# Moving a background matrix-vector product to other units of a hand-scheduled transformer kernel

## The chip, the core and the metric

The kernel runs on one core of one Trainium2 chip. The metric is device time in microseconds (us) of one execution, taken as the median of three runs. A profiled execution has a time of its own, and a span from its first to its last instruction.

## What is computed

Two transformer blocks run over 256 tokens of width 2048, all in float32. The first has a stick-breaking attention layer and a latent attention layer. The second has a gated convolution, a sparse attention that picks 64 keys for each query, and a feed-forward part. The second block is modulated by six vectors that depend on a condition `c` alone:

```
mod = silu(c) @ w_ada + b_ada                    # w_ada is 2048 x 12288
sh1, sc1, gt1, sh2, sc2, gt2 = split(mod, 6)
h = rms_norm(x, g_pre_mix) * (1 + sc1) + sh1     # then the projections, convolution, attention
x = x + gt1 * rms_norm(mixed, g_post_mix)
h = rms_norm(x, g_pre_ffn) * (1 + sc2) + sh2     # then the feed-forward part
x = x + gt2 * rms_norm(f, g_post_ffn)
```

The modulation needs nothing of the token stream, so its 100 MB of weights can be read at any time before the vectors are used.

## The kernel before, in words

**Units.** The class `Run` writes out the whole program in the order of units. A unit (`u`) is 6 matmuls of 128x128 by 128x512 on the TensorE (PE) for one half `t` of the tokens: each weight is split into a high and a low part, and two slices of 128 rows take three matmuls each. A block is 512 columns of one weight matrix, 16 units where it has 2048 rows. `pump` brings weights in, up to 10 units ahead: SyncE (SP) issues a load of 512 KB into one of 4 buffers `wst` for each two units, ScalarE (ACT) makes the high part `wh` and VectorE (DVE) the low part `wl` (L213 and L214, or L227 and L228 where a gain is folded in). There are 6 buffers of `wh` and of `wl`, so a `wl` can be made at most 12 units ahead of the matmuls that read it.

**Side work.** After each unit `side` advances generators that hold everything else: norms, transposes (L522, which DVE and ACT then split into `h` and `l` tiles such as `ah` and `al`), attention heads, the convolution. A generator's `yield n` says that its next piece is written n units later. Each engine runs its own instructions strictly in the order of writing, so what is written first also waits first.

**The modulation products.** At the end of `side` stands the modulation. It has 384 slices of `w_ada` (128 rows by 512 columns, 256 KB). GpSimd (POOL) issues the load of one into one of 3 buffers `ast` (L329), and DVE multiplies it with one value of silu(c) for each row and adds it to `ada` (L571, or L568 for the first of 16). After 16 slices `ada_sum` adds up the partitions: ACT and DVE split `ada` into `adh` and `adl`, and 5 units later PE multiplies them with ones (L588, L589). `spread` gives each slice a due unit, evenly over the units that it calls calm: away from the turns between stages (`turns`) and from a stretch named by `heads`. Of the 384 slices, 320 have their place ahead of the feed-forward part. In `side`, one unit uses a slice or begins a load, not both (`elif`), and a load begins only when one of the three buffers has been used.

**Stages, in order of time.** First layer's projections and stick-breaking heads (units 0 to 271), output projection `w_out_a` (272 to 335), a turn with the short matrix `w_ple_proj` and then `w_ple_gate` (336 to 407); the latent stage with `w_dkv`, `w_in_b`, and the pairs `w_uk`, `w_uv`, `w_uq` with latent attention (408 to 575); `w_out_b` and the second turn of that kind (576 to 711); the second block's `w_in` with convolution and sparse attention (712 to 1111), `w_o` (1112 to 1175), and the feed-forward part. At the entries to the second block and to the feed-forward part, `affine` turns the normed rows of each half into the transposed activation, four pieces of 512 columns for each half, in `to_c` and `to_f`.

**Places that the change touches.** `side`; `mix_sums`, called in `out_phase`, which forms three sums for the norm after `w_o` (L556 on ACT, L1692 on DVE, L1693 on ACT); `to_c`; `conv`, 31 DVE operations for each of 8 groups of channels (L1393, L1396), written four at a time with 3 units between; `spread`.

Of the kernel before, what the change touches and what calls it, by code (L numbers as in the profile page):

```python
# [29 lines left out]
XBUF = 3  # L30
# [4 lines left out]
CONV_PACE = 3  # L35
# [100 lines left out]
class Run:  # L136
# [170 lines left out]
    def side(self):  # L307
        for rec in list(self.urgent):
            if not rec[2] and rec[1] <= self.u:
                self.advance(rec)  # L310
        for rec in self.slow:
            if rec[1] <= self.u:
                self.advance(rec)
        self.urgent, self.slow, self.active = ([r for r in x if not r[2]] for x in (self.urgent, self.slow, self.active))
        if (self.queue and len(self.active) < self.width and self.u >= self.last + self.space
                and all(r[2] for r in self.queue[0][3])):
            rec = self.queue.popleft()
            rec[1] = self.u
            self.active.append(rec)
            self.last = self.u  # L320
        self.step()
        if self.xc < self.xd and self.extra[self.xc][0] <= self.u:
            x = self.extra[self.xc]
            x[2](x[3])
            self.xc += 1
        elif (self.xd < len(self.extra) and self.xd - self.xc < XBUF and self.extra[self.xd][0] - 12 <= self.u):
            x = self.extra[self.xd]
            st = self.main.tile([P, NB], F32, tag="ast", bufs=XBUF, name="ast")
            self.nc.gpsimd.dma_start(st, x[1])  # L329
            x.append(st)  # L330
            self.xd += 1
# [111 lines left out]
def body(ctx, tc, a, out):  # L443
# [192 lines left out]
    blocks = []  # L636
# [278 lines left out]
    def out_phase(w, act_in, begin, src, act_next, then, sums=None, last_groups=None):  # L915


        def enter():
            st["x"], st["og"], st["oss"] = {}, {}, {}
            begin()  # L920
            for t in range(2):
                st["x"][t] = ph.tile([P, D], tag="x", bufs=2)
                nc.gpsimd.dma_start(st["x"][t], src(t))

        def epi_of(j):
            def epi(t, acc):
                if j == 0:
                    st["og"][t] = wide()
                    st["oss"][t] = small(ph.pool, 12, "oss")
                square(acc, st["oss"][t][:, j : j + 1])  # L930
                sl = slice(j * NB, (j + 1) * NB)
                nc.vector.tensor_tensor(st["og"][t][:, sl], acc, st["gp"][:, sl], op=ALU.mult)
                if sums is not None:
                    sums(t, j, st["og"][t][:, sl])
                if j == 3:

                    def fin():
                        r = rstd_of(ph.pool, total(ph.pool, st["oss"][t][:, 0:4]), D)
                        x = st["x"][t]

                        def update(g):
                            s2 = slice(g * NB, (g + 1) * NB)
                            nc.vector.scalar_tensor_tensor(x[:, s2], st["og"][t][:, s2], r, x[:, s2],
                                                           op0=ALU.mult, op1=ALU.add)
                            return x[:, s2]

                        yield from then(t, r, update)

                    run.advance(run.add(fin(), act_next, t))
                yield 1  # L950

            return epi

        for j in range(4):
            add_block(w, (0, D), j * NB, NB, act_in, epi_of(j), spare=j > 0 or act_in is not actB2,
                      groups=last_groups if j == 3 else None, enter=phase("po", enter) if j == 0 else None)
# [373 lines left out]
    def to_c(t, j, x):  # L1330
# [3 lines left out]
        if j == 3:  # L1334
            if t == 0:
                gain_of(0, "mix")
            x, xn = st["x"][t], wide()
            r = rstd_of(ph.pool, total(ph.pool, st["xss", t]), D)

            def norm(g):  # L1340
                sl = slice(g * NB, (g + 1) * NB)
                nc.vector.tensor_scalar(xn[:, sl], x[:, sl], r, None, op0=ALU.mult)
                return xn[:, sl]

            yield from affine(t, actC, 0, norm, *TO_C[t])
# [45 lines left out]
    def conv(c):  # L1391
        u, acc = st["uT"][:, c, :], st["cacc"][:, c, :]
        nc.vector.tensor_scalar(acc, u, wdw[:, c, 30:31], col("bdw", c), op0=ALU.mult, op1=ALU.add)  # L1393
        for k in range(29, -1, -1):
            sft = 30 - k
            nc.vector.scalar_tensor_tensor(acc[:, sft:], u[:, : S - sft], wdw[:, c, k : k + 1], acc[:, sft:],  # L1396
                                           op0=ALU.mult, op1=ALU.add)
            if k % 4 == 0:
                yield CONV_PACE

    def conv_chain(j, before):
        while not all(r[2] for r in before):
# [460 lines left out]
    def spread(run):  # L1863
# [1 line left out]
        uf = blocks[n_ffn].u0  # L1865
        calm = lambda lo, hi: [u for u in range(lo, hi) if all(not b - 12 <= u < b + 20 for b in turns)
                               and not heads[0] - 4 <= u < heads[-1] + 4]
        heads = [b.u0 for b in blocks if b.w.tensor.name in (a["w_uk"].tensor.name, a["w_uq"].tensor.name)]
        turns = [b.u0 for b in blocks if b.enter is not None or b.ahead is not None or b.w.tensor.name == a["w_ple_proj"].tensor.name]
        xs = []  # L1870
        uc = conv_block.u0
        for qs, us in ((range(20), calm(100, uc - 30) + calm(uc + 290, uf - 110)), (range(20, 24), calm(uf + 40, uf + 300))):
            todo = [(q, k) for q in qs for k in range(16)]
            for i, (q, k) in enumerate(todo):
                xs.append([us[len(us) * i // len(todo)], *ada_chunk(q, k)])
# [53 lines left out]
```

## Time and profile before

| | before |
|---|---|
| median of 3 runs | 2538.36 us (2535.8 to 2538.81) |
| profiled execution's own time | 2536.7 us |
| its span | 2534.9 us |
| PE busy | 2471.3 us, 97% |
| DVE busy | 1814.5 us, 72% |
| ACT busy | 1329.5 us, 52% |
| POOL busy | 283.6 us, 11% |
| mean granted TensorE clock | 0.994 |

Busy is the time in which an engine has an instruction running. The ends of matmuls are modelled and overlap, so a busy PE says that no gap was seen, and what a stage could gain is read from PE's gaps and from the stretches at the lower clock. Waits are put down to the instruction that came last.

### The profile page before, as it was taken

To read this page: it belongs to the slowest core of one execution; us is meant where nothing else is said; L and a number is where in the kernel's file an instruction comes from. 1 tells how busy PE (TensorE), PEld (TensorE's weight loads), DVE (VectorE), ACT (ScalarE), POOL (GpSimd) and SP (SyncE) were. 2 spreads that over 40 slices of the span, in tenths; PEclk is the share of its full clock that TensorE was granted. 3 is DMA by queue.
4 is the path that set the end of the run, shared out by engine and by line. 5 is a ranking of instruction groups with operands and counts; after the bars stand their busy time and mean duration, and the time that the engine had idled before them with its cause. 6 is when DMAs were issued, how large, how long until landed. Compare 5 with 4: busy or idle time off the path is not lost.

```text
span 2534.9 us, 33034 instructions
## 1 busy us (share of the span) xinstructions
PE 2471.3 (97%) x11818; PEld 2051.2 (81%) x11818; DVE 1814.5 (72%) x2492; ACT 1329.5 (52%) x1938; POOL 283.6 (11%) x535
## 2 busy tenths in 40 slices
PE   9999999999899999999999999999999999999998
PEld 7888888878689887878977877888788878888886
DVE  5466677787776667767999867675776787776665
ACT  6555564455555555554544465445644554455453
POOL 2011112112213401000000001100000000000000
PEclk9999999999999999999999999999999999999999
DMA  7577778887786667756656547875577767656563
GB/s 250 172 237 251 253 233 297 283 270 247 264 277 193 195 220 250 230 194 191 188 150 198 176 150 225 286 257 192 176 265 259 238 200 269 223 181 228 184 202 126
DMA packets 272213, 562.51 MB, mean 222 GB/s; under 512 B 20984, under 2 KB 43928, under 8 KB 270000
## 3 DMA queue, kind: packets, MB, share of 16 engines
q1 hardware_dynamic: 236688, 438.56, 53.6%
q0 software_dynamic: 34448, 120.67, 13.9%
q8 instruction: 93, 1.52, 0.2%
q10 hardware_dynamic: 912, 1.17, 0.1%
q14 instruction: 72, 0.59, 0.1%
HBM read 551.86 MB, written 8.45 MB: 221 GB/s over the span
## 4 chain that ended last, share of the span: by engine, by line
PE 85%; DVE 6%; DMA 3%; ACT 2%; issue 2%; POOL 1%; DVEq 0%; POOLq 0%; SPq 0%; ACTq 0%
PE acc L421 17%; PE acc L423 17%; PE acc L422 17%; PE acc L344 7%; PE sc L421 5%; PE sc L423 5%; PE sc L422 5%; PE sc L344 4%; PE pv L344 3%; DVE wl L214 2%; DMA ast<-in_w_ada_dram 2%; PE sc L1205 1%; PE tp L522 1%; ACT wh L213 1%; PE pv L1205 1%
## 5 line engine op out<-in xcount | busy, mean ns | idle before, releaser
L214 DVE TENSOR_TENSOR wl<-wst,wh 128x1024 fp32r<-128x1024 f32 (+2 forms) x758 | 904.3, 1198 | 447.8 <-ACT wh L213 444.6
L213 ACT ACTIVATE wh<-wst 128x1024 fp32r<-128x1024 f32 (+2 forms) x758 | 783.8, 1038 | 728.1 <-PE acc L423 289.2
L421 PE MATMUL acc<-wh,ah 128*128 128x512 f32 (+4 forms) x1630 | 639.8, 393 | 5.6 <-ACT wide L1600 2.9
L422 PE MATMUL acc<-wl,ah 128*128 128x512 f32 (+4 forms) x1630 | 628.0, 385 | 1.5 <-DVE wl L214 1.5
L423 PE MATMUL acc<-wh,al 128*128 128x512 f32 (+4 forms) x1630 | 627.5, 385 | 1.9 <-DVE sst L551 1.9
L329 POOL DMA_DIRECT2D ast<-in_w_ada_dram x384 | 207.7, 541 | 1514.5 <-DVE ada L571 1262.6
L421 PEld LDWEIGHTS acc<-wh,ah 128*128 128x128 f32 x1630 | 308.9, 190 | 64.7 <-ACT wide L1600 3.4
L423 PEld LDWEIGHTS acc<-wh,al 128*128 128x128 f32 x1630 | 308.5, 189 | 62.2 <-DVE al L527 2.1
L422 PEld LDWEIGHTS acc<-wl,ah 128*128 128x128 f32 x1630 | 309.1, 190 | 57.1 <-DVE wl L214 3.3
L571 DVE SCALAR_TENSOR_TENSOR ada<-ast,silu_c,ada 128x512 f32<-128x512 f32 x360 | 268.2, 745 | 61.8 <-DMA ast<-in_w_ada_dram 61.7
L1396 DVE SCALAR_TENSOR_TENSOR cv<-cv,wdw 128x255 f32<-128x255 f32 (+14 forms) x240 | 112.3, 468 | 6.5
L344 PE MATMUL acc<-wh,ah 128*128 128x512 f32 x270 | 105.6, 391 | 0.0
L344 PE MATMUL acc<-wh,al 128*128 128x512 f32 x270 | 105.1, 389 | 0.0
L344 PE MATMUL acc<-wl,ah 128*128 128x512 f32 x270 | 105.1, 389 | 0.0
L421 PE MATMUL sc<-wh,ah 128*128 128x512 f32 x266 | 104.7, 394 | 0.0
L422 PE MATMUL sc<-wl,ah 128*128 128x512 f32 x266 | 103.7, 390 | 0.0
L423 PE MATMUL sc<-wh,al 128*128 128x512 f32 x266 | 103.7, 390 | 0.0
L227 ACT ACTIVATE wh<-wst,cols 128x512 fp32r<-128x512 f32 (+2 forms) x112 | 68.3, 663 | 43.5 <-PE acc L423 27.5
L228 DVE SCALAR_TENSOR_TENSOR wl<-wst,cols,wh 128x512 fp32r<-128x512 f32 (+2 forms) x112 | 72.2, 688 | 13.8 <-ACT wh L227 13.7
L421 PE MATMUL sc<-wh,hh 128*128 128x512 f32 x176 | 68.9, 391 | 0.0
L421 PE MATMUL acc<-wh,hh 128*128 128x512 f32 x176 | 68.8, 391 | 0.0
L423 PE MATMUL acc<-wh,hl 128*128 128x512 f32 x176 | 68.5, 389 | 0.0
(440 smaller groups left out, 3892.1 us busy)
## 6 DMA issues: line engine op xcount, KB each, us to landing
ast<-in_w_ada_dram POOLq DMA_DIRECT2D x384, 256.0 KB, 4.2
wst<-in_w_in_dram SPq DMA_DIRECT2D x144, 512.0 KB
wst<-in_w_in_a_dram SPq DMA_DIRECT2D x120, 512.0 KB
wst<-in_w_down_dram SPq DMA_DIRECT2D x88, 512.0 KB
wst<-in_w_gate_dram SPq DMA_DIRECT2D x70, 512.0 KB
wst<-in_w_up_dram SPq DMA_DIRECT2D x70, 512.0 KB
wst<-in_w_ple_gate_dram SPq DMA_DIRECT2D x64, 512.0 KB
wst<-in_w_in_b_dram SPq DMA_DIRECT2D x40, 512.0 KB
```

The costliest lines, as they stand in the source:

```text
L213: nc.scalar.activation(wh, st, AF.Copy)
L214: nc.vector.tensor_sub(wl, st, wh.bitcast(F32))
L227: nc.scalar.activation(wh[:, c, :], st[:, c, :], AF.Copy, scale=g)
L228: nc.vector.scalar_tensor_tensor(wl[:, c, :], st[:, c, :], g, wh[:, c, :].bitcast(F32), op0=ALU.mult, op1=ALU.subtract)
L329: self.nc.gpsimd.dma_start(st, x[1])
L344: nc.tensor.matmul(banks[x], lhsT=l, rhs=r[:, c, :], start=new and c == k == 0, stop=stop and c == 1 and k == 2, skip_group_check=True)
L421: nc.tensor.matmul(o, lhsT=hi, rhs=wh[:, c, :], start=kc == 0, stop=False)
L422: nc.tensor.matmul(o, lhsT=hi, rhs=wl[:, c, :], start=False, stop=False)
L423: nc.tensor.matmul(o, lhsT=lo, rhs=wh[:, c, :], start=False, stop=kc == b.cp * b.np - 1)
L571: nc.vector.scalar_tensor_tensor(acc, w, s, acc, op0=ALU.mult, op1=ALU.add)
L1205: nc.tensor.matmul(o, lhsT=l, rhs=r, start=start, stop=True, skip_group_check=True)
L1396: nc.vector.scalar_tensor_tensor(acc[:, sft:], u[:, : S - sft], wdw[:, c, k : k + 1], acc[:, sft:], op0=ALU.mult, op1=ALU.add)
```

## The change

Five places change. `side` may use a slice and begin a load in one unit. `spread` counts the whole latent stage, from `w_dkv` on, as not calm (before, only from `w_uk` on), and lets the products begin at unit 66 in place of 100. In `out_phase` and in `to_c`, the last piece of the second half's sums is written one unit later. `conv` writes two operations at a time, with 2 units and 1 unit between in turn.

```
 in side:
             x[2](x[3])
             self.xc += 1
-        elif (self.xd < len(self.extra) and self.xd - self.xc < XBUF and self.extra[self.xd][0] - 12 <= self.u):
+        if (self.xd < len(self.extra) and self.xd - self.xc < XBUF and self.extra[self.xd][0] - 12 <= self.u):
...
 in out_phase:
                 if sums is not None:
+                    if j == 3 and t == 1:
+                        yield 1
                     sums(t, j, st["og"][t][:, sl])
...
 in to_c:
             if t == 0:
                 gain_of(0, "mix")
+            else:
+                yield 1
...
 in conv:
-            if k % 4 == 0:
-                yield CONV_PACE
+            if k % 2 == 0:
+                yield 2 if k % 4 == 0 else CONV_PACE - 2
...
 in spread:
-        heads = [b.u0 for b in blocks if b.w.tensor.name in (a["w_uk"].tensor.name, a["w_uq"].tensor.name)]
+        heads = [b.u0 for b in blocks if b.w.tensor.name in (a["w_dkv"].tensor.name, a["w_uq"].tensor.name)]
...
-        for qs, us in ((range(20), calm(100, uc - 30) + calm(uc + 290, uf - 110)), (range(20, 24), calm(uf + 40, uf + 300))):
+        for qs, us in ((range(20), calm(66, uc - 30) + calm(uc + 290, uf - 110)), (range(20, 24), calm(uf + 40, uf + 300))):
```

With the constants of the kernel, `spread` has 406 calm units for the 320 slices before and 376 after. They are, after: 66 to 259, 292 to 323, 362 to 395, 560 to 563, 596 to 627, 666 to 681, 1002 to 1065. Before, the list began at 100 and also held 428 to 491. Since a use and a load took a unit each, the program before could place one slice in two units only, and it fell behind its due units by up to 91 of them; after the change each slice stands in its due unit.

DVE at the entry of the latent stage, before: the weights of `w_dkv` (L228), the last update of `x` by the gate (L977, L978), the split of the transposed `x` (L527) and the statistics of the next norm (L551, L542).

```order
L977 TENSOR_TENSOR nat<-nat,big 128x512
L978 TENSOR_TENSOR x<-x,nat 128x512
L571 SCALAR_TENSOR_TENSOR ada<-ast,silu_c,ada 128x512
L228 SCALAR_TENSOR_TENSOR wl<-wst,cols,wh 128x320 x2
L527 TENSOR_TENSOR al<-tp,ah 128x512
L571 SCALAR_TENSOR_TENSOR ada<-ast,silu_c,ada 128x512
L228 SCALAR_TENSOR_TENSOR wl<-wst,cols,wh 128x320 x2
L551 TENSOR_REDUCE sst_5550<-xss_4812 128x1
L542 TENSOR_SCALAR var_5552<-sst_5550 128x1
L527 TENSOR_TENSOR al<-tp,ah 128x512
```

The same place now (line numbers behind L329 are 2 to 4 higher):

```order
L979 TENSOR_TENSOR nat<-nat,big 128x512
L980 TENSOR_TENSOR x<-x,nat 128x512
L228 SCALAR_TENSOR_TENSOR wl<-wst,cols,wh 128x320 x2
L527 TENSOR_TENSOR al<-tp,ah 128x512
L228 SCALAR_TENSOR_TENSOR wl<-wst,cols,wh 128x320 x2
L551 TENSOR_REDUCE sst_5829<-xss_5105 128x1
L542 TENSOR_SCALAR var_5831<-sst_5829 128x1
L527 TENSOR_TENSOR al<-tp,ah 128x512
```

The products (L571) no longer stand between the steps that lead to the latent stage; no L571 stands on DVE from there to the last of `w_uq`.

DVE in the middle of `w_out_a`, before, where a product stands behind each `wl`:

```order
L571 SCALAR_TENSOR_TENSOR ada<-ast,silu_c,ada 128x512
L214 TENSOR_TENSOR wl<-wst,wh 128x1024
L585 TENSOR_TENSOR adl<-ada,adh 128x256
L571 SCALAR_TENSOR_TENSOR ada<-ast,silu_c,ada 128x512
L214 TENSOR_TENSOR wl<-wst,wh 128x1024
L571 SCALAR_TENSOR_TENSOR ada<-ast,silu_c,ada 128x512
L214 TENSOR_TENSOR wl<-wst,wh 128x1024
```

And now:

```order
L585 TENSOR_TENSOR adl<-ada,adh 128x256
L571 SCALAR_TENSOR_TENSOR ada<-ast,silu_c,ada 128x512 x2
L214 TENSOR_TENSOR wl<-wst,wh 128x1024
L571 SCALAR_TENSOR_TENSOR ada<-ast,silu_c,ada 128x512 x2
L214 TENSOR_TENSOR wl<-wst,wh 128x1024
L571 SCALAR_TENSOR_TENSOR ada<-ast,silu_c,ada 128x512
L214 TENSOR_TENSOR wl<-wst,wh 128x1024
```

Most `wl` now have two products between them. ACT at the entry of the feed-forward part, before: the second half's sums (L556 of `sc`, L556 of `wide`, L1693) and the first half's second and third piece of `affine` (L1316, L1319).

```order
L556 ACTIVATE junk,oss_15567<-sc 128x512
L556 ACTIVATE junk,oss_15567<-wide 128x512
L1693 ACTIVATE nat,oss_15567<-nat 128x512
L1316 ACTIVATE nat<-tp,mods,gsc 128x128 x4
L1319 ACTIVATE ah<-nat 128x512
L213 ACTIVATE wh<-wst 128x1024 x2
L1316 ACTIVATE nat<-tp,mods,gsc 128x128 x4
```

And now:

```order
L556 ACTIVATE junk,oss_15567<-sc 128x512
L1318 ACTIVATE nat<-tp,mods,gsc 128x128 x4
L1321 ACTIVATE ah<-nat 128x512
L213 ACTIVATE wh<-wst 128x1024
L556 ACTIVATE junk,oss_15567<-wide 128x512
L1697 ACTIVATE nat,oss_15567<-nat 128x512
L213 ACTIVATE wh<-wst 128x1024
L1318 ACTIVATE nat<-tp,mods,gsc 128x128 x4
```

The two sums went from ahead of the second piece to between the second and the third.

## Rows read from the trace of the kernel before

**Rows 1.** The page: each engine's busy time, its share of the span, instructions.

```profile
PE 2471.3 (97%) x11818; PEld 2051.2 (81%) x11818; DVE 1814.5 (72%) x2492; ACT 1329.5 (52%) x1938; POOL 283.6 (11%) x535
```

**Rows 2.** Stretches: us, busy of PE, PEld, DVE, ACT, POOL, clock, DMA share, GB/s.

```profile
600.00:900.00 300.00, 280.83 (x1685) 247.53 (x1684) 199.98 (x366) 168.14 (x354) 87.10 (x170) 0.98 0.70 223
650.00:700.00 50.00, 43.01 (x177) 34.37 (x178) 36.91 (x72) 29.70 (x66) 14.64 (x33) 0.90 0.76 248
437.00:492.00 55.00, 55.00 (x247) 45.57 (x247) 41.23 (x52) 25.14 (x36) 10.23 (x19) 1.00 0.93 335
492.00:523.00 31.00, 27.17 (x133) 21.36 (x132) 24.52 (x36) 18.60 (x30) 5.73 (x11) 1.00 0.65 214
990.00:1016.00 26.00, 21.50 (x106) 16.89 (x105) 23.04 (x34) 17.14 (x26) 5.27 (x9) 1.00 0.69 233
1250.00:1350.00 100.00, 100.00 (x483) 79.14 (x482) 92.54 (x193) 47.61 (x70) 0.00 (x0) 1.00 0.55 163
1350.00:1360.00 10.00, 7.06 (x24) 5.39 (x24) 9.68 (x17) 5.16 (x6) 0.00 (x0) 0.83 0.67 206
```

**Rows 3.** PE's waits from 600 to 900 us: total, times, longest.

```profile
PE acc L421 <- DVE kT L1124: 3.6, 4, 1.3
PE tp L522 <- DVE ckvl L535: 2.5, 1, 2.5
PE acc L423 <- DVE sst L551: 1.9, 1, 1.9
```

**Rows 4.** DVE in order of time: start, length; in brackets idle time before, and releaser.

```profile
626.20 0.75 DVE L571 SCALAR_TENSOR_TENSOR ada<-ast,silu_c,ada 128x512 f32<-128x512 f32 x1 [5.79 <-DMA ast<-in_w_ada_dram]
...
628.04 0.68 DVE L527 TENSOR_TENSOR al<-tp,ah 128x512 fp32r<-128x512 f32 x1
...
640.25 0.75 DVE L571 SCALAR_TENSOR_TENSOR ada<-ast,silu_c,ada 128x512 f32<-128x512 f32 x1 [1.14 <-DMA ast<-in_w_ada_dram]
```

**Rows 5.** POOL in order of time, 618 to 642 us.

```profile
618.11 0.54 POOL L986 DMA_DIRECT2D spill<-x  x1 [0.81 <-DVE x L978]
618.64 0.55 POOL L329 DMA_DIRECT2D ast<-in_w_ada_dram  x1
...
641.30 0.54 POOL L329 DMA_DIRECT2D ast<-in_w_ada_dram  x1 [2.61 <-DVE ada L571]
```

**Rows 6.** The chain, in order of time: one load of a slice, and 6 matmuls.

```profile
618.64 7.46 DMA ast<-in_w_ada_dram
...
1886.50 1.36 PE sc L344 x6
```

**Rows 7.** Products from 611 to 870 us, and DVE's idle time before them.

```profile
L571 DVE SCALAR_TENSOR_TENSOR ada<-ast,silu_c,ada x71: 736/745/760, 612.5 to 868.9; 128x512 f32<-128x512 f32 x71
...
  DMA ast<-in_w_ada_dram: 44.0, 16
```

**Rows 8.** PE's waits over the whole span, one row.

```profile
PE tp L522 <- DVE x L943: 5.5, 6, 1.2
```

**Rows 9.** Loads of slices from 700 to 740 us, from issue to landing.

```profile
DMA to landing us min/median/max: 3.6/4.2/5.4
```

**Rows 10.** Products and loads of slices from 454 to 480 us.

```profile
L571 DVE SCALAR_TENSOR_TENSOR ada<-ast,silu_c,ada x12: 742/746/752, 454.3 to 478.8; 128x512 f32<-128x512 f32 x12
...
DMA to landing us min/median/max: 4.0/5.2/6.0
```

**Rows 11.** One of DVE's groups from 437 to 492 us: busy, mean, idle before.

```profile
L571 DVE SCALAR_TENSOR_TENSOR ada<-ast,silu_c,ada 128x512 f32<-128x512 f32 x19 | 14.2, 747 | 9.0 <-DMA ast<-in_w_ada_dram 9.0
```

**Rows 12.** Products from 144 to 397 us.

```profile
L571 DVE SCALAR_TENSOR_TENSOR ada<-ast,silu_c,ada x75: 736/745/752, 145.9 to 391.6; 128x512 f32<-128x512 f32 x75
```

**Rows 13.** Entry of the feed-forward part, in order of time: ACT twice, then PE.

```profile
1791.40 0.63 ACT L556 ACTIVATE junk<-wide 128x512 bf16<-128x512 f32 x1 [2.92 <-DVE wide L932]
...
1792.76 1.49 ACT L1316 ACTIVATE nat<-tp,mods,gsc 128x128 f32<-128x128 f32 x4
...
1794.96 0.50 PE L421 MATMUL acc<-awh,ah 128*128 128x512 f32 x1 [3.38 <-ACT ah L1319]
```

More of the change, by code (lines that the diff above doesn't have):

```diff
@@ L325, in side @@
             self.xc += 1
-        elif (self.xd < len(self.extra) and self.xd - self.xc < XBUF and self.extra[self.xd][0] - 12 <= self.u):
+        if (self.xd < len(self.extra) and self.xd - self.xc < XBUF and self.extra[self.xd][0] - 12 <= self.u):
             x = self.extra[self.xd]
@@ L933, in epi @@
                 if sums is not None:
+                    if j == 3 and t == 1:
+                        yield 1
                     sums(t, j, st["og"][t][:, sl])
@@ L1336, in to_c @@
                 gain_of(0, "mix")
+            else:
+                yield 1
             x, xn = st["x"][t], wide()
@@ L1397, in conv @@
                                            op0=ALU.mult, op1=ALU.add)
-            if k % 4 == 0:
-                yield CONV_PACE
+            if k % 2 == 0:
+                yield 2 if k % 4 == 0 else CONV_PACE - 2
     def conv_chain(j, before):
@@ L1867, in spread @@
                                and not heads[0] - 4 <= u < heads[-1] + 4]
-        heads = [b.u0 for b in blocks if b.w.tensor.name in (a["w_uk"].tensor.name, a["w_uq"].tensor.name)]
+        heads = [b.u0 for b in blocks if b.w.tensor.name in (a["w_dkv"].tensor.name, a["w_uq"].tensor.name)]
         turns = [b.u0 for b in blocks if b.enter is not None or b.ahead is not None or b.w.tensor.name == a["w_ple_proj"].tensor.name]
@@ L1871, in spread @@
         uc = conv_block.u0
-        for qs, us in ((range(20), calm(100, uc - 30) + calm(uc + 290, uf - 110)), (range(20, 24), calm(uf + 40, uf + 300))):
+        for qs, us in ((range(20), calm(66, uc - 30) + calm(uc + 290, uf - 110)), (range(20, 24), calm(uf + 40, uf + 300))):
             todo = [(q, k) for q in qs for k in range(16)]
```

## The prediction

> **What bounds the kernel now.** I read the page first: PE has an instruction running in 97% of the span, no other engine in more than 72% [rows 1]. So time can come back only where PE has gaps or runs at the lower clock. The view of stretches shows where these are. From 600 to 900 us, the latent stage, PE is busy for 280.83 of 300 us, a gap of 19.2 us, and between 650 and 700 us the granted clock is 0.90, so 10 of these 50 us ran at the lower of the two levels and 5.0 us of work were lost [rows 2]. Two more gaps lie at the turns to `w_ple_proj`: 31.00 - 27.17 = 3.8 us and 26.00 - 21.50 = 4.5 us [rows 2]. A matmul stretch without a gap looks like 437 to 492 us, 55.00 of 55.00 [rows 2].
>
> The list of PE's waits says what ends the gaps in the latent stage. The longest is for `kT`, a copy on DVE, then for the split of the normed latent (`ckvl`) and for the statistics of the next norm (`sst`), DVE again [rows 3]. The order of time on DVE and POOL shows why DVE is late. At 618.11 us POOL issues the write of `x` (the spill), for which it had waited; the load of a slice stood behind it and goes out at 618.64 us [rows 5]. It takes 7.46 us to land [rows 6]. DVE stands at the product for 5.79 us, and the split `al` that PE needs, long since ready to run, begins at 628.04 us [rows 4]. Over the whole stage DVE runs 71 products and waits 44.0 us for 16 late loads [rows 7]. DVE isn't busy there; it is held up.
>
> **What the change removes.** The 71 products and their loads leave the latent stage, and with them the 44.0 us of waiting on DVE, the PE matmuls that sum up finished columns, and the slice loads among POOL's rope and norm steps. The wait rows for `kT`, `ckvl` and `sst` add up to 8.0 us; the rest of the 19.2 us is spread over shorter waits, of which I put about 3 us down to the stage's own chains (the attention pairs at its end, where no product runs). I take 14 of the 19.2 us as gone, and 4 of the 5.0 us of clock, since the low clock follows on the gaps: 18 us. The bounds are 8 us (the three named waits alone) and 24.2 us (all of it).
>
> At the two turns the same pattern stands: PE's transposes wait 5.5 us in six places for `x`, the update on DVE [rows 8], which has products in front of it. The change keeps products 12 units before and 20 units after a turn, now in fact, since none is overdue. I take 6 of 3.8 + 4.5 = 8.3 us, between 2 us (what the `x` row would leave if only a third of it were the products') and 8.3 us. Together 24 us return, between 10 and 32.5.
>
> **What it adds.** The products that are due ahead of the feed-forward part now stand in 376 units, 320/376 = 0.851 for each, in place of 0.5, the most that the old rule let through. Three things are paid.
>
> DVE's own time: in pure matmul stretches a unit lasts 1.36 us [rows 6]. From 437 to 492 us DVE is busy for 41.23 of 55 us at about 0.5 products a unit [rows 2]; 0.35 more at 0.745 us each add 0.26 us to 1.02 us a unit, which stays under 1.36. DVE isn't the bound.
>
> The loop of three buffers: a load waits for the product that frees its buffer, so three products take one landing, one product, and the gaps between them. The product of 640.25 us ends at 641.00 and POOL issues at 641.30 [rows 4, 5]: 0.30. The load issued at 618.64 with 7.46 lands at 626.10, the product starts at 626.20 [rows 4, 6]: 0.10. With 0.745 for the product itself [rows 7], a product takes at best (landing + 1.14)/3. Needed is one in 1.36/0.851 = 1.60 us. At 288 GB/s or so landings have a median of 4.2 us [rows 9], which gives 1.78 us; where the loads came thick, 5.2 us [rows 10], which gives 2.11 us (there, 11 gaps in 24.5 us were 2.2 us each). So the loop is too slow in pure stretches by 0.18 to 0.51 us a product, and DVE falls behind, with the weight splits behind it in its queue.
>
> What hides it: a `wl` is written 10 units ahead of its use, 13.6 us. That cover is shown to work. From 437 to 492 us DVE waited 9.0 us for slices [rows 11] and PE was busy for 55.00 of 55.00 us [rows 2]. I count 9 us as free in each stretch, and take the landing midway, 4.7 us (load thickens the traffic to somewhere between the two rows), so 1.95 us and a lag of 0.35 us a product. The stretch of 64 units (1002 to 1065) has 54 products: 18.9 us of lag, 9 free, 10 us paid. The two stretches of 32 units have 27 each: 9.4 us, hidden. Those of 34 and 16 units stay under 9 as well. The long stretch 66 to 259 contains attention heads, and its units are longer: 75 products, with some 5 first ones between them, 79 gaps of two units in 245.7 us [rows 12], 1.555 us a unit, 1.83 us a product. It has fewer weight bytes a us, so I use 4.2 us there, 1.78, no lag. Sum: 10 us. The bounds are 0 (4.2 us everywhere: 54 x 0.18 = 9.7, as good as hidden) and 65 us (5.2 us everywhere: 18.5 + 2 x 4.8 + 165 x 0.28 - 9 = 37).
>
> The convolution: a group of 31 operations now takes 23 units, not 24. DVE is busy for 92.54 of 100 us from 1250 to 1350 and has just let PE run dry behind it, 2.9 us of gap and a clock of 0.83 [rows 2]. By unit 888, where that gap lies, 7 operations more will have been written, of which half fall into the saturated stretch: 3.5 x 0.5 = 1.7 us; the 0.5 is an estimate between half and all of the product's 0.745 us [rows 7], which has twice the columns. I take 2 us, between 0 (even spacing gives as much back) and 3.5.
>
> **Edits that I cost at nothing.** At the entry of the feed-forward part PE waits 3.38 us for the second piece of the first half; ACT works on the second half's sums from 1791.40 until that piece begins at 1792.76 [rows 13]. Now the piece goes first and can come 1.2 us sooner. But the sums then stand ahead of the third piece, which ends when it ended before, and PE waits for that in its place. The second half's own rows have 8 units of cover. The same holds in `to_c`. I take 0, between +1.2 and -1.2 us at each of the two places.
>
> **Sum.** The profiled execution took 2536.7 us (span 2534.9); the median of the runs is 2538.4, and the difference of 1.7 us is carried over. -24 + 10 + 2 + 0 = -12 us: 2526 us.
>
> **Rivals.** *The dense stretches are free.* If landings stay near 4.2 us, or the cover is longer than 9 us, nothing of the 10 us is paid, and if the stage's gaps go almost entirely, 30 us return: 2508 us. For it speaks the row of 4.2 us; against it the 5.2 us at close spacing. The Trainium skill, DMA: Bandwidth & Descriptors, section on the anatomy of one DMA on the gpsimd path, puts such a load at about 2.0 us plus its bytes over 436 GB/s, 2.6 us for 256 KB, an estimate by that page; the loop would then need 1.25 us, below 1.60, and this rival would hold. The trace doesn't agree: no load in the two rows landed in under 3.6 us.
>
> *The gaps in the latent stage are its own.* Then norm, rope and transposes bind PE as the products did, only 10 us come back and the 12 us are paid: 2540 us, no change that can be told. For it speaks that the stage has short blocks and long chains; against it the 44.0 us that DVE stood still.
>
> *The loop of three buffers becomes the bound* (the slower side). DVE stands at a product as it does in the latent stage now, but in five stretches, and the heads of the first layer, with 4 units between their steps, wait with it. At 5.0 us of landing, 2.05 us a product, the stretches cost 15 + 2 x 3 + 165 x 0.22 - 9 = 27, together 48 us: 2538.4 - 24 + 48 + 2 = 2564 us. It outweighs the gain from about 4.8 us on. For it speaks the median of 5.2 us; against it that those loads ran while the weight buffers were being filled again after a stall.
>
> **How the numbers follow.** Forecast 0.42, free 0.26, own gaps 0.17, loop 0.15. About 0.2%, 5 us, is what a measurement of this kernel tells from no change. Faster by more than that: the free case and nearly all of the forecast, 0.67. Within it: 0.18, the own gaps and an edge of the others. Slower: 0.15. The likeliest is 2526 us, itself between 2518 and 2533. The range for 8 in 10 goes from the free case, 2508, to the loop case at a lesser landing, 2547.
>
> **What will show it.** Right: from `w_dkv` to `w_uq` no DVE idle time is put down to a slice, PE's gap in that stage falls from 19.2 to about 5 us and its clock stays at 1.0; at the turns DVE's `x` is no longer waited for; in the dense stretches DVE's idle time for slices grows, most in 1002 to 1065, and PE shows some 10 us of gaps there; landings have a median of 4.5 to 5. Near unit 888 the gap is up by 2 us. Wrong: if the gap in the latent stage stays over 10 us, the first term has failed; if PE has no gap in the dense stretches, the cover was underrated; if it has over 25 us, the loop is the bound.

## The result and the profile after

The changed kernel takes 2555.37 us (median of 4 runs, 2552.96 to 2560.76), the kernel before 2537.14 us beside it: a ratio of 1.0075, 95% interval 1.0063 to 1.0087. It is slower by 0.75%, where the prediction said 0.5% faster. The profiled execution took 2552.96 us, span 2551.2 us.

PE is busy in as large a share as before [rows 1], but the span is 16.3 us longer. This is the busy line of the page of the changed kernel:

```profile
PE 2476.7 (97%) x11818; PEld 2051.4 (80%) x11818; DVE 1813.9 (71%) x2492; ACT 1325.8 (52%) x1938; POOL 290.3 (11%) x535
```

To see where it went, the same work must be laid beside the same work. The rows below are stretches between the first matmuls of units 64, 264, 336, 360, 408 and 576, then of the second turn (units 640 to 663), and then between those of units 1000, 1112, 1176 and 1216. Before (the columns are those of [rows 2]):

```profile
84.40:403.10 318.70, 316.84 (x1530) 265.35 (x1529) 208.36 (x254) 182.96 (x246) 44.65 (x83) 1.00 0.74 233
403.10:505.70 102.60, 101.63 (x462) 83.99 (x460) 74.32 (x91) 47.97 (x66) 21.64 (x40) 1.00 0.84 294
505.70:546.00 40.30, 36.98 (x175) 29.46 (x174) 34.91 (x46) 24.21 (x34) 8.09 (x15) 1.00 0.82 271
546.00:615.60 69.60, 69.60 (x323) 57.44 (x322) 59.09 (x84) 40.14 (x69) 11.83 (x22) 1.00 0.80 260
615.60:907.20 291.60, 272.43 (x1653) 240.57 (x1652) 193.23 (x347) 164.95 (x340) 84.95 (x166) 0.98 0.69 220
...
999.10:1039.00 39.90, 37.13 (x179) 30.13 (x178) 28.92 (x37) 23.37 (x33) 2.72 (x5) 1.00 0.66 217
...
1535.10:1696.00 160.90, 160.90 (x741) 132.28 (x740) 120.76 (x152) 75.92 (x100) 25.28 (x47) 1.00 0.79 259
...
1786.80:1853.70 66.90, 61.83 (x274) 49.15 (x273) 51.92 (x78) 37.81 (x60) 3.85 (x7) 0.97 0.61 206
```

And the same units after:

```profile
82.90:427.20 344.30, 328.32 (x1553) 272.09 (x1552) 264.95 (x348) 188.07 (x268) 91.24 (x167) 0.98 0.84 280
427.20:529.70 102.50, 101.57 (x457) 83.30 (x456) 69.71 (x83) 47.72 (x64) 15.84 (x29) 1.00 0.78 269
529.70:568.10 38.40, 37.17 (x180) 30.25 (x179) 26.36 (x34) 23.55 (x35) 2.15 (x4) 1.00 0.66 216
568.10:646.80 78.70, 71.55 (x317) 58.66 (x316) 62.16 (x87) 39.38 (x66) 13.94 (x26) 0.96 0.75 238
646.80:913.20 266.40, 262.19 (x1634) 234.85 (x1632) 143.51 (x263) 159.11 (x322) 49.63 (x93) 1.00 0.54 169
...
1006.70:1044.00 37.30, 36.45 (x176) 29.73 (x174) 25.77 (x31) 22.81 (x32) 2.15 (x4) 1.00 0.67 218
...
1540.40:1707.40 167.00, 163.17 (x744) 132.52 (x743) 123.39 (x157) 75.58 (x101) 27.46 (x51) 1.00 0.76 256
...
1797.60:1870.00 72.40, 63.63 (x276) 48.44 (x275) 52.04 (x78) 38.20 (x60) 4.79 (x7) 0.98 0.59 190
```

The latent stage (fifth row) is 25.2 us shorter: PE's gap in it fell from 19.2 to 4.2 us, the clock went from 0.98 to 1.00. But the first layer (units 64 to 263) is 25.6 us longer, `w_ple_gate` (360 to 407) 9.1, the sparse attention's stretch (1000 to 1111) 6.1, and the entry of the feed-forward part (1176 to 1215) 5.5.

What PE waits for in the first layer, in the list of its waits from 60 to 430 us, after:

```profile
PE tp L522 <- DVE wide L891: 7.2, 3, 4.9
PE sc L850 <- ACT sph L846: 5.1, 3, 2.3
PE pv L834 <- ACT e L855: 2.3, 1, 2.3
```

Before, only the last of these had been there (1.7 us). None is a wait for `wl`. (In the sparse attention's stretch it is not a `wl` either: nearly all of PE's gap of 3.8 us there goes to the modulation's own column sums.)

```profile
PE tp L589 <- DVE adl L585: 3.6, 3, 2.3
```

L891 multiplies a head's output by its gate, and `yield 2` later PE transposes it (L522); L846 is the step of a head that PE reads 4 units after it was written. DVE's waits from 130 to 425 us say what held these steps up; and under them the landings of slices there (least, median, most us):

```profile
DVE ada L571 <- DMA ast<-in_w_ada_dram: 41.6, 36, 2.5
DVE ada L568 <- PE tp L604: 8.6, 2, 6.0
...
DMA to landing us min/median/max: 2.9/3.9/5.2
```

There are two holds. The first is the slice that has not landed. DVE in order of time near 325 us:

```profile
323.68 1.54 DVE L571 SCALAR_TENSOR_TENSOR ada<-ast,silu_c,ada 128x512 f32<-128x512 f32 x2
325.13 1.22 DVE L214 TENSOR_TENSOR wl<-wst,wh 128x1024 fp32r<-128x1024 f32 x1
326.27 0.75 DVE L571 SCALAR_TENSOR_TENSOR ada<-ast,silu_c,ada 128x512 f32<-128x512 f32 x1
328.67 0.75 DVE L571 SCALAR_TENSOR_TENSOR ada<-ast,silu_c,ada 128x512 f32<-128x512 f32 x1 [1.66 <-DMA ast<-in_w_ada_dram]
329.34 1.22 DVE L214 TENSOR_TENSOR wl<-wst,wh 128x1024 fp32r<-128x1024 f32 x1
330.48 0.55 DVE L844 SCALAR_TENSOR_TENSOR e<-sc,e 128x384 f32<-128x384 f32 x1
```

L844, a head's step whose input ACT had finished at 325.5 us, stands behind the products and a `wl` until 330.48. Of these 5.0 us 1.66 are the wait for the slice, and the rest is DVE's work, put off, it seems, by earlier waits. Then ACT makes `sph`, and PE, empty since its matmul of 328.94, goes on at 331.64 (PE's order of time):

```profile
328.94 0.39 PE L423 MATMUL acc<-wh,al 128*128 128x512 f32 x1
331.64 0.44 PE L850 MATMUL sc<-sph,tri 128*128 128x384 f32 x1 [2.31 <-ACT sph L846]
```

The second hold is new and has nothing to do with loads. Finished columns leave one of two accumulators `ada`. A fourth column keeps its accumulator until PE's L604 has transposed its rows, by the `yield`s of `ada_sum` 3 + 5 + 1 + 5 + 1 + 4 + 5 = 24 units after its last product. The column after next begins 17 products later: 34 units at the old half a unit, 20 units at 0.85. So its first product, L568, stands 4 units. DVE near 382 us:

```profile
374.80 1.23 DVE L214 TENSOR_TENSOR wl<-wst,wh 128x1024 fp32r<-128x1024 f32 x1
382.05 0.49 DVE L568 TENSOR_SCALAR ada<-ast,silu_c 128x512 f32<-128x512 f32 x1 [6.03 <-PE tp L604]
...
387.65 0.68 DVE L891 TENSOR_TENSOR wide<-wide,nat 128x512 f32<-128x512 f32 x1
```

PE waits 4.87 us for that L891, and the clock follows on this gap and those ahead of it. From 350 to 400 us it is 0.90, 10 of 50 us at the lower of the two levels (columns as in [rows 2]):

```profile
350.00:400.00 50.00, 42.27 (x185) 34.00 (x185) 35.73 (x49) 28.17 (x37) 11.08 (x21) 0.90 0.73 234
```

### The profile page after: what moved, and what is told of

Read it like the earlier page. It is cut to its first block, busy times and chain, and to the rows that moved or that the text cites. A ratio compares the mean times of both kernels' runs of the same rounds, so it can differ in the third digit from the quotient of the medians.

```text
span 2551.2 us, 33059 instructions
## 1 busy us (share of the span) xinstructions
PE 2476.7 (97%) x11818; PEld 2051.4 (80%) x11818; DVE 1813.9 (71%) x2492; ACT 1325.8 (52%) x1938; POOL 290.3 (11%) x535
## 5 line engine op out<-in xcount | busy, mean ns | idle before, releaser
L329 POOL DMA_DIRECT2D ast<-in_w_ada_dram x384 | 208.4, 543 | 1346.6 <-DVE ada L571 1170.5
L571 DVE SCALAR_TENSOR_TENSOR ada<-ast,silu_c,ada 128x512 f32<-128x512 f32 x360 | 269.5, 748 | 99.4 <-DMA ast<-in_w_ada_dram 97.1
L228 DVE SCALAR_TENSOR_TENSOR wl<-wst,cols,wh 128x512 fp32r<-128x512 f32 (+2 forms) x112 | 71.7, 688 | 46.9 <-ACT wh L227 46.8
L421 PE MATMUL acc<-wh,hh 128*128 128x512 f32 x176 | 68.8, 391 | 0.0
```

The costliest lines, as they stand in the source:

```text
L228: nc.vector.scalar_tensor_tensor(wl[:, c, :], st[:, c, :], g, wh[:, c, :].bitcast(F32), op0=ALU.mult, op1=ALU.subtract)
L421: nc.tensor.matmul(o, lhsT=hi, rhs=wh[:, c, :], start=kc == 0, stop=False)
L571: nc.vector.scalar_tensor_tensor(acc, w, s, acc, op0=ALU.mult, op1=ALU.add)
```

## Experiments

The times are medians; each ratio is to the kernel before, run on the same chip, with its 95% interval. The kernel before took 2535.1 to 2537.1 us beside the several groups of runs, so a difference between groups is known to some 2 us.

**Are late slices the cause?** The product reads a tile that is always there.

```
+            w = mean_c[:, None, :].to_broadcast([P, 4, P])
```

> The changed kernel, but the product multiplies a tile that is always there (mean_c, repeated four times) in place of the slice just loaded, so the modulation vectors are not the reference's; the 384 loads, the products' count and their length stay. Theory A, late slices: in the changed kernel DVE stands 41.6 us for slices between 130 and 425 us, and the heads' steps and the gate's products queue behind it; without that wait most of the 34 us lost in units 88 to 264 and 376 to 399 comes back, about 25: 2530 us. Theory B, DVE's own time (more products between the heads' steps): nothing comes back, 2553 to 2556 us. Theory C, the two accumulators: the first product of a column still stands for PE's L604 (8.6 us on DVE), so the gap of 5.0 us at 383 us stays, and little comes back: 2545 to 2550 us.

Measured: 2524.85 us, 0.9961 (0.9948 to 0.9973). Some 30 us come back, by theory A; a third of it in the first layer, a third in `w_ple_gate`. Units 64 to 263 take 333.9 us, in place of 344.4; a part of what is left there shows on DVE from 130 to 425 us (lines are one higher in this kernel):

```profile
DVE ada L569 <- PE tp L605: 14.1, 2, 8.1
```

This is the accumulators' wait, now longer, since DVE comes earlier to it.

**The accumulators alone.**

```
 in ada_sum, for a fourth column:
-        yield 4
+        yield 1
...
-        yield 5
+        yield 3
```

> The changed kernel with 5 units less between a fourth column's row and PE's transpose L604 that frees its accumulator (1 and 3 units in place of 4 and 5). Theory C, the two accumulators: the waits of 6.0 and 2.6 us on L604 go, with the PE gap of 5.0 us before L522 at 383 us and its clock, 8 to 12 us: 2543 to 2547 us. Theory A: at most the 5.0 us gap, 2549 to 2552 us. If neither wait matters, 2555 us.

Measured: 2555.47 us, 1.008 (1.0068 to 1.0093): no change. Theory C alone falls. DVE's wait for L604 is gone, but its wait for slices from 130 to 425 us rises from 41.6 to 46.4 us, and PE now waits at L604 itself, for the rows that are read back from memory (its row over the whole span):

```profile
DVE ada L571 <- DMA ast<-in_w_ada_dram: 46.4, 45, 2.6
...
PE tp L604 <- DMA ada<-mod: 7.3, 4, 4.1
```

So the total hides two parts: the first layer and `w_ple_gate` are 3.4 and 2.6 us shorter than in the changed kernel, and units 336 to 359 and 576 to 711 are 1.6 and 4.4 us longer.

**Out_phase and the convolution.** Each undone by itself.

```
 e1_noout, in out_phase:
-                    if j == 3 and t == 1:
-                        yield 1
 e1_noconv, in conv:
-            if k % 2 == 0:
-                yield 2 if k % 4 == 0 else CONV_PACE - 2
+            if k % 4 == 0:
+                yield CONV_PACE
```

> The changed kernel without the extra unit in out_phase. If that unit costs the 5 us that PE loses at the entry of the feed-forward part (1.1 us at unit 1176, 4.2 at 1184): 2550 us. If the loss comes from products or from chance, no change: 2555 us.

> The changed kernel with the convolution four operations at a time, as before. By the prediction's term the change costs 2 us: 2553 us. By the trace, in which the gap at unit 888 is as long as before (3.14 against 3.10 us): 2555 us, within 1 us.

Measured: 2550.06 us, 1.0058 (1.0045 to 1.007), so the extra unit in `out_phase` costs 5 us; and 2554.84 us, 1.0075 (1.0062 to 1.0089), so the convolution's edit costs nothing that can be told. PE's waits at the entry of the feed-forward part: after from 1797 to 1870 us, then `e1_noout` from 1800 to 1867.

```profile
PE acc L421 <- ACT ah L1321: 4.3, 2, 2.5
PE sc L421 <- ACT ah L1321: 3.3, 4, 0.9
```

```profile
PE acc L421 <- ACT ah L1319: 4.4, 2, 3.4
```

The longest wait shrinks from 3.4 to 2.5 us, as predicted for the first half's piece. But the second half's four pieces (the matmuls into `sc`) now come late as well, 3.3 us in sum.

**A fourth slice buffer.** First the control that makes room for it, then the buffer.

```
-XBUF = 3
+XBUF = 4
```

> The changed kernel with memory freed for a fourth slice buffer, which is not used yet: three buffers nat in place of four in the first layer, the second block and the feed-forward part, and the convolution's taps of two groups of channels standing for all eight, so its result is not the reference's. The control for the next run. Expected: 2555 us; up to 2560 where the third nat buffer was needed.

> The control with four slice buffers (XBUF 4), the convolution's taps as there. Theory A1, the loop of three buffers: with four, a product needs (3.95 + 1.14)/4 = 1.27 us and more than the 1.60 us wanted in pure matmul stretches is at hand, so DVE's wait for slices between 130 and 425 us falls from 41.6 us to under 10 and 20 to 28 us come back against the control: 2530 us. Theory A2, the transfers' rate (the DMA rows show 300 GB/s there; a fourth load only waits longer to land): landings rise to 5.5 us and more, and under 8 us come back: 2547 us or more.

Measured: 2561.62 us, 1.0095 (1.008 to 1.0111), and with the buffer 2523.62 us, 0.9958 (0.9946 to 0.997): 38 us less than the control, and some 30 us less than the changed kernel (the control lies some 5 us above that, where no change was expected; their intervals overlap). DVE's waits from 130 to 425 us with four buffers, and the landings:

```profile
DVE ada L568 <- PE tp L604: 14.2, 2, 8.1
DVE ada L571 <- DMA ast<-in_w_ada_dram: 9.8, 14, 1.9
...
DMA to landing us min/median/max: 2.9/4.5/7.9
```

Landings rise only to 4.5 us, so the transfers' rate (A2) was not the limit; the number of buffers was (A1).

**The same slices over more units.**

```
-calm(66, uc - 30) + calm(uc + 290, uf - 110)
+calm(54, uc - 30) + calm(uc + 290, uf - 30)
```

> The changed kernel with the 320 slices spread over more units: from 54 on in place of 66, and up to 30 units ahead of the feed-forward part in place of 110, 439 units, so 0.73 a unit in place of 0.85; one each 1.87 us in a pure matmul stretch. Theory A1: that is more than the 1.75 us which the loop needs, so no lag gathers between the heads: DVE's wait for slices hardly matters to PE, and about 20 of the 30 us come back: 2535 us. Theory A2, and any theory by which each late slice costs its own part: the loss shrinks with the number in the first layer (150 for 165): 2550 us.

> e2_wide, and out_phase without its extra unit, and the accumulator freed 5 units sooner as in e1_short. By theory A1 with the 5 us of out_phase: 2528 us, less than either kernel. Where the accumulators' wait has come to bear now that DVE is not late otherwise, up to 6 us lower. If the density was not the cause: 2545 us.

Measured: 2515.53 us, 0.9918 (0.9905 to 0.9931), faster than both kernels and 20 us below what A1 said. One reason is that at 0.73 the accumulators come free nearly in time as well (17 products take 23 units; of that wait 2.5 us are left). Slices are still late in the first layer, but PE waits there for none of the steps behind them. DVE from 60 to 425 us:

```profile
DVE ada L571 <- DMA ast<-in_w_ada_dram: 18.7, 27, 1.8
```

`e2_best` gives 2515.11 us, 0.9919 (0.9906 to 0.9931): its two further edits do not show in the total. `e2_wide` in the first layer, `w_ple_gate` and the stretch from 1000 on:

```profile
84.60:407.00 322.40, 320.49 (x1551) 267.62 (x1550) 252.70 (x325) 188.63 (x265) 79.74 (x146) 1.00 0.85 282
...
544.90:615.20 70.30, 69.73 (x322) 57.14 (x321) 59.32 (x85) 40.61 (x70) 11.80 (x22) 1.00 0.77 251
...
1504.80:1669.50 164.70, 162.89 (x748) 132.85 (x747) 136.67 (x177) 77.05 (x105) 38.59 (x72) 1.00 0.86 293
```

**Where between 0.73 and 0.85 does it turn?** In one kernel with the last slices 76 units ahead of the feed-forward part in place of 110 (0.78 a unit), in the other with the slices of the first layer even in time.

```
 e3_middle:
-calm(uc + 290, uf - 110)
+calm(uc + 290, uf - 76)
 e3_even:
+            us = [u for u in us for _ in range(10 if u > 264 else 11 if u // 8 % 6 in (2, 3, 4) else 9)]
```

> The changed kernel with the units up to 76 ahead of the feed-forward part in place of 110: 410 units, 0.78 a unit, one each 1.74 us in a pure matmul stretch, 152 of them before unit 264, as many as in e2_wide (there from 54 on, here from 66 on). Theory A1, a threshold where the loop of three just keeps up ((4.0 + 1.14)/3 = 1.71 us by the page's landing, 1.81 by the spacing seen in the changed kernel): between the two, 2525 to 2540 us. If only the number of slices in the first layer counted: as e2_wide, 2516 us. If the density counts evenly: 0.78 lies 0.07 below 0.85 and 0.05 above 0.73, 2532 us.

> The changed kernel with as many slices in each calm stretch (166 before unit 264), but in the first layer placed evenly in time and not in units: 9 parts of weight for a unit of a pure matmul piece, 11 for a unit of the pieces with attention heads, which last longer. 0.77 a unit in pure pieces, one each 1.78 us. By the theory that DVE falls behind in the pure pieces and the heads at their end pay for it: 12 to 20 of the 25.7 us lost in units 88 to 264 come back, 2535 to 2543 us. If it is the mean density, or the heads' own products: no gain, 2555 us or more, since heads have more of them beside them now.

Measured: `e3_middle` 2534.06 us, 0.9992 (0.9982 to 1.0002), half of the way. DVE's wait for slices from 60 to 425 us lies between those of the two kernels, at 32.6 us, and so does the accumulators' wait, at 5.6 us; so this run does not say which of the two holds set the time.

```profile
DVE ada L571 <- DMA ast<-in_w_ada_dram: 32.6, 32, 3.2
```

`e3_even` gives 2553.13 us, 1.007 (1.0056 to 1.0084), hardly a gain. Thinner slices in the pure pieces, paid for with denser ones beside the heads, do not help; which of the two places lags by itself is not shown by it.

**Both holds at once.** `e2_x4` and `e3_even`, each with the accumulator freed 5 units sooner.

> e2_x4 (four slice buffers; taps of two groups of the convolution for all eight) with the accumulator freed 5 units sooner, as in e1_short. If the accumulators' wait for L604 (14.2 us on DVE with four buffers, PE gaps of 2.5 and 4.5 us and the lower clock behind them) is what is left: 10 to 14 us come back, 2510 to 2514 us. If the rest is the heads' own products or DVE's time: 2522 to 2524 us.

> e3_even (slices of the first layer evenly in time) with the accumulator freed 5 units sooner. If lag in the pure pieces and the accumulators are two causes that stand in for each other, neither cure alone shows (2553 and 2555 us), but both together do: 2538 to 2545 us. If the mean density or the products beside the heads decide: 2550 us or more.

Measured: 2524.88 us, 0.9949 (0.9937 to 0.9962), and 2560.18 us, 1.0085 (1.0071 to 1.01). Neither total moves down. By place the first does: units 64 to 263 take 326.8 us in place of 335.3, and PE's wait for L891 falls (from 60 us to the end of the layer, `e2_x4`, then `e4_x4short`; under them the first layer of `e4_x4short`).

```profile
PE tp L522 <- DVE wide L891: 5.2, 2, 4.4
...
PE tp L522 <- DVE wide L891: 0.8, 1, 0.8
...
84.90:411.70 326.80, 322.67 (x1554) 270.10 (x1553) 267.28 (x348) 189.65 (x268) 91.46 (x167) 0.99 0.87 294
```

It is given back, for PE now meets L604 before its rows have been read back, as in `e1_short` (waits of `e4_x4short` over the whole span):

```profile
PE tp L604 <- DMA ada<-mod: 4.6, 4, 1.7
```

Units 336 to 407 and 576 to 711 lose 4.5 and 3.1 us by it (and the start, ahead of any product, took 2.7 us longer in this execution). So the accumulators' wait is worth 8.5 us in the first layer with four buffers, and this way of taking it away costs about as much. For slices even in time the joint cure brought nothing, 339.9 us both times: with 0.94 slices a unit beside the heads, DVE waits 53.8 us for slices from 60 to 430 us.

**Was it right to clear the latent stage?** `e2_wide` with units 428 to 491 allowed again; and that with the old rule for loads.

```
-if all(not b - 12 <= u < b + 20 for b in turns)
+if 428 <= u < 492 or all(not b - 12 <= u < b + 20 for b in turns)
```

> e2_wide with units 428 to 491 of the latent stage counted as calm again, so 43 slices are used between units 404 and 575 (3 in e2_wide, 79 in the kernel before), and fewer elsewhere. If taking the products out of the latent stage is what gave the changed kernel about 25 us there: 40 of 76 slices bring some half of it back as a loss, 9 to 13 us: 2525 to 2528 us. If that stage's gaps are its own: 2515 us, or a little less, since the other stretches are thinner.

> e3_latent with the old rule for loads (one unit uses a slice or begins a load), so that nearly every load is written one unit ahead of its product: 31 slices in units 408 to 487 and 12 in 488 to 575 (38 and 5 in e3_latent). If early loads are what keeps the latent stage whole: its 19 us come back in good part, 8 to 16 us of loss for 43 of 77 slices, and the turns lose 2 us each: 2523 to 2533 us. If the number of products in the stage decides: no more than 2516 us.

Measured: 2513.3 us, 0.9912 (0.9897 to 0.9926), and 2519.69 us, 0.993 (0.9919 to 0.9942). The stage takes 269.0 us with 43 slices (266.6 with 3 in `e2_wide`), and 272.7 us with 43 under the old rule, against 291.6 with 78 in the kernel before (products that begin between units 404 and 575). So half of the slices cost a tenth to a quarter of the loss, not a half. The old rule costs 6.4 us by the medians, and the two intervals still overlap; by place it loses 3.7 us in this stage and 3.2 in the turn (units 336 to 359).

**The unit in to_c, and what helps put together.** `e3_notoc` is `e2_wide` without the unit; the others leave out that of `out_phase`.

> e2_wide without the extra unit in to_c. If that unit gave the 1.9 us by which the gap near unit 712 is shorter in the changed kernel: 2517 to 2518 us. Otherwise 2515.5 us, within 1 us.

> e3_latent without the extra unit in out_phase, and with the last slices 76 units ahead of the feed-forward part: 0.66 a unit. The stage at the entry of the feed-forward part loses 4.3 us less, as in e1_noout: 2509 us. If the thinner placing or the unit's gain do not add up: 2513 us.

> e2_wide without the extra unit in out_phase. If that unit's price adds up: 4 us less than e2_wide, 2511 us, less than either kernel. If something else ends the entry of the feed-forward part there (the last columns' sums, now close ahead of it): 2515 us.

> e3_latent without the extra unit in out_phase: 43 slices between units 404 and 575. If the unit's price adds up: 2509 us. Against e5_wide_noout: if products in the first part of the latent stage are nearly free at 0.64 a unit, equal or 2 us less; if they cost 5 to 8 us, as in e4_best, 2 to 5 us more.

Measured, in this order: 2517.68 us, 0.9929 (0.9917 to 0.9941); 2514.07 us, 0.991 (0.9898 to 0.9923); 2513.58 us, 0.9914 (0.9899 to 0.9929); 2508.26 us, 0.9889 (0.9873 to 0.9906). The unit in `to_c` is worth some 2 us by the medians, which is less than the intervals tell apart; by place it is 1.6 to 1.8 us, for units 700 to 719 take 36.1 us before and 36.2 in `e3_notoc`, 34.3 after and 34.6 in `e2_wide`. The last is the best kernel, 1.1% under the kernel before. Three of its stretches, the first layer, the latent stage with its 43 slices, and the entry of the feed-forward part:

```profile
83.30:405.70 322.40, 320.56 (x1545) 268.21 (x1544) 240.21 (x303) 186.97 (x260) 68.12 (x127) 0.99 0.82 267
...
612.50:881.60 269.10, 264.11 (x1646) 236.22 (x1644) 170.33 (x309) 161.97 (x332) 72.23 (x133) 1.00 0.64 206
...
1759.80:1826.80 67.00, 61.96 (x276) 49.36 (x275) 52.04 (x78) 37.92 (x60) 3.84 (x7) 0.97 0.62 206
```

The lengths of the main stretches in one table (us, from the first matmul of one unit to that of the other; the last column is the median of the runs):

| kernel | slices a unit | 64-263 | 360-407 | 408-575 | 1000-1111 | 1176-1215 | time |
|---|---|---|---|---|---|---|---|
| before | 0.5 | 318.7 | 69.6 | 291.6 | 160.8 | 66.9 | 2537.1 |
| after | 0.85 | 344.4 | 78.8 | 266.4 | 167.0 | 72.3 | 2555.4 |
| e1_fixed | 0.85 | 333.9 | 68.8 | 266.4 | 161.5 | 71.0 | 2524.9 |
| e1_short | 0.85 | 341.0 | 76.2 | 266.4 | 167.2 | 71.1 | 2555.5 |
| e2_x4 | 0.85 | 335.3 | 71.9 | 266.4 | 161.3 | 71.0 | 2523.6 |
| e4_x4short | 0.85 | 326.8 | 74.7 | 266.5 | 161.7 | 71.0 | 2524.9 |
| e3_middle | 0.78 | 328.7 | 77.0 | 266.2 | 170.2 | 72.3 | 2534.1 |
| e2_wide | 0.73 | 322.4 | 70.3 | 266.6 | 164.7 | 71.1 | 2515.5 |
| e3_latent | 0.64 | 322.4 | 68.7 | 269.0 | 162.7 | 72.1 | 2513.3 |
| e4_best | 0.66 | 321.5 | 69.2 | 274.5 | 161.5 | 67.0 | 2514.1 |
| e5_latent_noout | 0.64 | 322.4 | 68.7 | 269.1 | 162.3 | 66.9 | 2508.3 |

## Why the prediction was wrong

**The term that failed** is "dense stretches, 10 us", and in it the step "The long stretch 66 to 259 ... no lag". It cost 25.6 us, and the dense stretches in all 25.6 - 0.1 + 9.1 + 6.1 = 40.7 us. PE's gaps in them are 16.0 + 0.9 + 7.2 + 3.8 = 27.9 us, beyond the 25 that the prediction named as the sign that the loop is the bound. With -25.2 us in the latent stage, -4.5 at the turns and 5.5 at the entry of the feed-forward part that makes 16.5 of the span's 16.3 us. Three things in that step were wrong, and the size of a landing was not among them: at 3.9 us it was even less than the 4.2 us used there. With that the loop needs (3.9 + 1.14)/3 = 1.68 us a product, and 1.83 us were at hand on the mean.

First, "What hides it: a `wl` is written 10 units ahead": that cover is real, and it was counted for the wrong instruction. In `w_out_a`, where it is mostly `wl` that stand behind the products, 0.85 a unit cost nothing (102.6 and 102.5 us). In the first layer PE waits for the heads' and gates' steps, written 2 or 4 units ahead, and in `w_ple_gate` for the update of `x`; these stand in the same queue on DVE. The rival of the loop named the heads, but priced the stretch against the same mean of 1.83 us a product, so at the landing of 3.9 us it has no lag there either. The units that were charged with 10 us, 1002 to 1065, lie in the stretch that lost 6.1, and there PE waited for the column sums, not for a `wl`.

Second, the best case of the loop was taken for what it does. By the table the first layer loses 3.7 us at 0.73 slices a unit and 10.0 at 0.78, that is at one product in 1.87 and in 1.74 us of pure matmuls, and DVE waits for slices at both (18.7 and 32.6 us), though 1.68 us is what the formula gives. A product also stands behind DVE's other work before it frees its buffer; that this is why is argued, not shown. That late slices are the main cause is shown from two sides: no wait for slices (some 30 us less), or a fourth buffer (38 us less than its control).

Third, the two accumulators were not looked at at all. "Each slice stands in its due unit" also means that the column after next begins 20 units after a column's last product, where 24 are needed. It is worth 8.5 us in the first layer where buffers are enough, and partly hidden behind the late slices where they are not; `e1_short` shows 3.4 us of it there, and gives it back at L604.

With both holds treated, 8.1 of the 25.6 us remain (`e4_x4short`): 2.3 us of PE's gaps (4.1 against 1.9) and 5.8 us of PE's busy time. Most of the latter is work that moved: at the same gap as before, `e2_wide` has 21 more matmuls in this stretch, all of them sums of finished columns, and 3.7 us more of busy time. The prediction counted such sums as leaving the latent stage and nowhere as arriving. What is left of the busy time goes with a clock of 0.99; slices even in time did not help as expected.

**The gain was right in place and about right in size**: -25.2 us in the latent stage, beyond the 18 and just past its bound of 24.2. Three products are left on DVE there, none waited for; PE's gap fell to 4.2 us where "about 5" was said, and the clock rose to 1.00. Of the three waits named in the prediction only 0.4 us for `ckvl` are left. Of the 25.2 us 15.0 are gap, and 10.2 are busy time: the clock, and by an estimate from the 21 matmuls above about 3 us for 19 matmuls that now run elsewhere. What it is owed to was told too simply. 43 slices in the first part of the stage cost 2.5 us at 0.64 a unit (two runs; 8 in `e4_best`). Before there were 78, not far from half of them overdue and running on into the attention pairs (36 begin from unit 488 on); as far as these runs show, most of the loss came with those. Clearing the stage was a way to be rid of these, and it pushed the density to 0.85; the kernel that leaves the first part open is 5 us faster than the one that clears it (2508.26 against 2513.58), and it is thinner elsewhere: units 64 to 263, 360 to 407 and 1000 to 1111 are 1.3, 2.0 and 3.7 us shorter in it. `e4_best` pays 8 us for about as many slices (44): PE's gap in the stage is 9.0 us there against 5.0 in `e5_latent_noout`, with two waits of 2.2 us (for `gate`, L610, and for `nat`, L1058) that the other does not have. Why they arise at this placing stays open.

**The turns**: predicted -6 us. The first gave 1.9 us and the second 2.6 (39.9 to 37.3 us), 4.5 in all; around the second the dense units take it back, and the stretch that holds it (576 to 711) is as long as before. PE's wait for that `x` fell from 5.5 us [rows 8] to 0.9, but PE waits for the update in `w_ple_gate` (L980) instead, which DVE reaches late:

```profile
PE tp L522 <- DVE x L980: 7.1, 2, 4.9
...
PE tp L522 <- DVE x L945: 0.9, 2, 0.5
```

**Convolution**: predicted +2 us, measured 0.5 us and within what can be told. The stretch around unit 888 (units 880 to 895) takes 26.8 us before and 26.5 after, so the gap there did not grow; that the even spacing is why is not shown. **Edits at nothing**: `to_c` gives some 2 us, as said. For `out_phase` the step "The second half's own rows have 8 units of cover" failed: it costs 5.3 us, since all four of that half's pieces now come late.

The time of 2564 us and the mechanism of the third rival came nearest, the time in part by luck: it rests on landings of 5.0 us that did not come. The Trainium skill, DMA: Bandwidth & Descriptors, section on the anatomy of one DMA on the gpsimd path, would have a 256 KB load land in an estimated 2.6 us; the loop would then need an estimated 1.25 us a product, and by the prediction's formula no stretch would have lagged. The trace doesn't agree: it says 3.9 us with three buffers and 4.5 us with four.

## What to carry to other kernels

When background work is packed denser, look at every ring that it turns, not only the buffer of its loads: for each one, compare the units from its last use to its release with the units until it is wanted again. The cover of a stretch is that of the instruction with the shortest lead in the queue that is held up, and not that of the commonest; a mean over a stretch says nothing of it. And when a change trades places for density, ask what density the ring can bear before choosing the places: here 0.73 a unit was worth 40 us against 0.85.

## What the runs showed that was not expected

How little a hold on one engine says of the time: DVE's 41.6 us of standing for slices in the first layer are worth 10.5 us of PE there (344.4 - 333.9), and a hold can be taken away without a trace in the total, because others fill its place (in `e1_short` 8.6 us for L604 went from DVE, 4.8 us more for slices came, and 7.3 us of waits at L604 came on PE). In `w_ple_gate` it was the other way: in `e1_fixed` some 10 us came back, of which only 7.2 had been gaps (78.70 - 71.55); the granted clock there was 0.96 after, and 1.00 in `e1_fixed`, where PE is busy for 68.80 of 68.80 us.
